# Gate and up blocks of four SwiGLU layers: seven half-size matrix products per pair in place of eight

## The chip, the cores and the metric

The kernel runs on one core of one Trainium2 chip. The metric is device time in microseconds (us), from the first to the last instruction of one execution and what lies around it; lower is better. The engines are called PE (TensorE's matrix products), PEld (its weight loads), DVE (VectorE), ACT (ScalarE), POOL (GpSimd) and SP (which only issues transfers here).

## What is computed

Two blocks of two layers each run one after the other on a sequence of 512 tokens with 1,024 features. Each of the four layers is a mixer (recurrent or attention), in the first block also a cross-attention to a memory, and a SwiGLU layer, each followed by a layer norm. The change touches the four SwiGLU layers alone:

```python
D_MODEL, SEQ, FFN_HIDDEN = 1024, 512, 2816

def swiglu(x, w_gu, w_down):
    gate, up = jnp.split(x @ w_gu, 2, axis=-1)
    return (jax.nn.silu(gate) * up) @ w_down

# in every layer
x = layer_norm(ALPHA * x + swiglu(x, w_gu[layer], w_down[layer]), g, b)
```

All arithmetic is to float32 accuracy.

## The kernel before

**Data.** Activations lie transposed: eight tiles of 128 features by 512 tokens (`XF` in float32, and the same split in two reduced-precision parts `XH` and `XL`, whose sum is `XF`). A gate or up block is 1,024 features by 128 outputs, 512 KB, stored as one 128 x 1024 tile: eight 128 x 128 pieces side by side, one for each tile of x. There are 22 gate and 22 up blocks in a layer (`FT`).

**A product.** `fetch` (L327 to L341) brings a block into `w_raw` (three buffers), ACT rounds it to `w_hi` (L337), and DVE subtracts to get `w_lo` in two halves of 512 columns (L339; four buffers each for `w_hi` and `w_lo`). `mm3` (L271 to L276) then makes three products: high by high, high by low, low by high. So one block is 8 x 3 = 24 matmuls of 128 x 128 by 512 tokens into one PSUM bank.

**A layer.** `ffn` (L549) goes in three parts of 8, 7 and 7 hidden tiles (`FPARTS`). For each hidden tile it computes the gate block into a bank with tag `mm`, the up block into one with tag `sc`, and then `evac`: ACT takes the Silu of gate (L564), DVE multiplies by up (L568), ACT and DVE split the result in `f_h` and `f_l` (L264, L266). Behind each part the down products of that part follow, eight blocks, and are added to `XF` (L404 to L409); those of the last part lie in `close_sublayer`, in two halves of 256 tokens, with the layer norm of the first half under the products of the second. The norm of the second half lies at the start of the next stage: in a SwiGLU layer its first two hidden tiles are computed in two halves of 256 tokens (`halves=True`), while the norm of tokens 256 to 511 is still being finished.

**Order.** The program says what depends on what; when it is built, the framework puts each engine's instructions into one queue, by when it expects them to be ready, and sets the waits between engines. A queue's order is therefore not the program's order, and it is fixed at run time. A buffer's next use waits for the last reader of its former content. `AO` is a scratch area of eight tiles; `close_sublayer` keeps the norm's sums and temporaries there (`room`).

Of the kernel before, what the change touches and what calls it, by code (L numbers as in the profile page):

```python
# [8 lines left out]
F32 = mybir.dt.float32  # L9
F32R = mybir.dt.float32r  # L10
U8 = mybir.dt.uint8
AF = mybir.ActivationFunctionType
ALU = mybir.AluOpType
# [3 lines left out]
P = 128  # L17
S = 512
D = 1024
KT = 8  # L20
# [33 lines left out]
def layout(i):  # L54
# [62 lines left out]
    for l in range(2):  # L117
        ffn(f"f{l}", f["ffn_w_gu"][l], f["ffn_w_down"][l])
        ffn(f"f{l + 2}", f["ffn_w13_2"][l], f["ffn_w2_2"][l])
# [55 lines left out]
def constants():  # L175
    c = {}
    idx = np.arange(P)
    eye = np.eye(P, dtype=np.float32)
    tri_le = (idx[:, None] <= idx[None, :]).astype(np.float32)
    neg_gt = np.where(idx[:, None] > idx[None, :], np.float32(1e30), np.float32(0))  # L180
    neg_lt = np.where(idx[:, None] < idx[None, :], np.float32(1e30), np.float32(0))
    neg_ge = np.where(idx[:, None] >= idx[None, :], np.float32(NEG), np.float32(0))
    tri_lt = (idx[:, None] < idx[None, :]).astype(np.float32)
    tri_ge = -(idx[:, None] >= idx[None, :]).astype(np.float32)
    c["c_sq"] = np.concatenate([eye, neg_gt, neg_lt, neg_ge, tri_lt, tri_ge], axis=1)

    inv = (np.float32(10000.0) ** (-np.arange(0, 64, 2, dtype=np.float32) / np.float32(64))).astype(np.float32)
    ang = np.arange(S, dtype=np.float32)[None, :] * inv[:, None]
    cos, sin = np.cos(ang).astype(np.float32), np.sin(ang).astype(np.float32)
    c["c_rope"] = np.concatenate(  # L190
        [np.concatenate([cos, cos, cos, cos]), np.concatenate([-sin, sin, -sin, sin])], axis=1
    )

    t = np.arange(P)
    lv = np.zeros((P, len(LEVELS), 64), np.float32)
    for n, h in enumerate(LEVELS):
        blk = t // (2 * h)
        right = (t // h) % 2
        lv[:, n, :] = (blk[:, None] == blk[right == 1][None, :]) & (right[:, None] == 0)
    c["c_lv"] = lv.reshape(P, len(LEVELS) * 64)  # L200
    rs = np.ones((P, S), np.float32)
    rs[:, ::64] = 0
    c["c_rs"] = rs
    return c


class Prog:
    def __init__(self, ctx, tc, a):
        self.tc, self.nc, self.a = tc, tc.nc, a
        nc = tc.nc  # L210
        self.cp = ctx.enter_context(tc.tile_pool(name="cst", bufs=1))
        self.st = ctx.enter_context(tc.tile_pool(name="state", bufs=1))
        self.wp = ctx.enter_context(tc.tile_pool(name="wts", bufs=4))
        self.ps = ctx.enter_context(tc.tile_pool(name="ps", bufs=4, space=PSUM))
        st = self.st
        xf = st.tile([P, KT * S], F32, name="xf")
        self.XF = [xf[:, k * S : (k + 1) * S] for k in range(KT)]
        self.all_x = xf.rearrange("p (k s) -> p k s", k=KT)
        self.XH = [st.tile([P, S], F32R, name=f"xh{k}") for k in range(KT)]
        self.XL = [st.tile([P, S], F32R, name=f"xl{k}") for k in range(KT)]  # L220
        self.AO = [st.tile([P, S], F32, name=f"ao{k}") for k in range(KT)]
        cp = self.cp

        ones = cp.tile([P, 2 * P], F32, name="k_ones")
        nc.vector.memset(ones[:, 0:P], 1.0 / D)
        nc.vector.memset(ones[:, P : 2 * P], 1.0 / P)
        self.ones_d, self.ones_p = ones[:, 0:P], ones[:, P : 2 * P]
        nr = cp.tile([P, P], F32R, name="k_nr")
        nc.vector.tensor_scalar(nr, ones[:, P : 2 * P], -float(P), None, ALU.mult)
        self.mones_r = nr  # L230
        pr = cp.tile([P, P], F32R, name="k_pr")
        nc.vector.tensor_copy(pr, ones[:, P : 2 * P])
        self.ones_pr = pr
        cc = cp.tile([P, 4], F32, name="k_cc")
        nc.vector.memset(cc[:, 0:1], LN_EPS)
        nc.vector.memset(cc[:, 1:2], 1.0)
        self.eps, self.one = cc[:, 0:1], cc[:, 1:2]
        self.kv = {}
        self.pending = []
        self.biases = []  # L240
        self.before = []
        self.loaded = False

    def constants(self):
        nc, a = self.nc, self.a
# [22 lines left out]
            y = nc.vector.scalar_tensor_tensor(lo, src, scale, hi.bitcast(F32), ALU.mult, ALU.subtract)  # L268
        return x, y

    def mm3(self, out, w, x, start, stop):  # L271
        nc = self.nc
        (wh, wl), (xh, xl) = w, x
        nc.tensor.matmul(out, wh, xh, start=start, stop=False)  # L274
        nc.tensor.matmul(out, wh, xl, start=False, stop=False)  # L275
        self.last = nc.tensor.matmul(out, wl, xh, start=False, stop=stop)  # L276

    def pair_parts(self, pool, name, width=S):

# [266 lines left out]
        self.close_sublayer(src, self.XH, self.XL, True, ln, keep=keep)  # L546


    def ffn(self, pre, ln, last=False):  # L549
        nc, tc, a = self.nc, self.tc, self.a  # L550
        with tc.tile_pool(name="ffn", bufs=2, reuse_waits="tile") as fp:
            off = 0
            for part, nt in enumerate(FPARTS):
                hs, ls = [], []
                for t in range(nt):
                    hs.append(fp.tile([P, S], F32R, name="f_h", tag="f_h", bufs=11))
                    ls.append(fp.tile([P, S], F32R, name="f_l", tag="f_l", bufs=11))

                def evac(n, ps, c0, c1, keep={}):
                    t = n // 2  # L560
                    c = slice(c0, c1)
                    if n % 2 == 0:
                        s = fp.tile([P, S], F32, name="f_s", tag="f_s", bufs=3)
                        nc.scalar.activation(s[:, c], ps[:, c], AF.Silu)  # L564
                        keep[t, c0] = s
                    else:
                        s = keep.pop((t, c0))
                        nc.vector.tensor_tensor(s[:, c], s[:, c], ps[:, c], ALU.mult)  # L568
                        self.tail = self.split(hs[t][:, c], ls[t][:, c], s[:, c])

                src = []
                for t in range(nt):
                    src += [a[pre + "_gu"][off + t], a[pre + "_gu"][FT + off + t]]
                if part == 0:
                    self.proj_a(src[:4], evac, halves=True)
                    self.proj_a(src[4:], lambda n, ps, c0, c1: evac(n + 4, ps, c0, c1), tags=("mm", "sc"))
                else:
                    self.proj_a(src, evac, tags=("mm", "sc"))
                off += nt
                d = a[f"{pre}_d{part}"]  # L580
                if part < len(FPARTS) - 1:
                    for m in range(8):
                        w = self.fetch(d[m], nt * P)
                        ps = self.mm(("mm", "sc")[m % 2])
                        self.block_a(w, ps, hs, ls)
                        self.add_partial(m, ps, part == 0)
                else:
                    self.close_sublayer([d[m] for m in range(8)], hs, ls, False, ln, last)


# [1011 lines left out]
```

## Time and profile before

| | |
|---|---|
| median of three runs | 2907.42 us (2905.26 to 2908.75) |
| the profiled execution | 2910.26 us, of which 2908.3 us are its span |
| PE busy | 2849.4 us, 98% of the span |
| weight loads (PEld) busy | 2415.0 us, 83% |
| DVE busy | 1694.3 us, 58% |
| ACT busy | 1274.8 us, 44% |
| POOL busy | 424.1 us, 15% |
| mean granted clock of TensorE | 0.996 of full speed |

The busy time of an engine is the time in which at least one of its instructions is running. A matmul's recorded duration is longer than the distance to the next one, since matmuls overlap: the pace is read from the distances between starts. Weight loads run beside the matmuls.

### The profile page before, as it was taken

What the parts mean: (1) busy time and instruction counts of PE and PEld (TensorE: products, weight loads), DVE (VectorE), ACT (ScalarE), POOL (GpSimd) and SP (SyncE); (2) the same over time, 40 slices, a digit from 0 to 9 for tenths busy, and PEclk for the clock granted to TensorE, in tenths of its full rate; (3) what the DMA queues carried; (4) which work ended last, traced back from release to release, by engine and by line L of the source; (5) the groups of instructions that cost most, each with busy time, mean ns of one, the idle gap of its engine ahead of it and who ended that gap; (6) DMA issues with size and microseconds to landing.
All of it is one profiled execution on the core that took longest, in us unless ns stands there. A gap on an engine that the chain in (4) does not pass through costs nothing.

```text
span 2908.3 us, 40029 instructions
## 1 busy us (share of the span) xinstructions
PE 2849.4 (98%) x15354; PEld 2415.0 (83%) x15354; DVE 1694.3 (58%) x3164; ACT 1274.8 (44%) x2328; POOL 424.1 (15%) x500
## 2 busy tenths in 40 slices
PE   9999999999999999999999999999999999999998
PEld 7678989888886678898888988798888976988887
DVE  5877656333469887563333767873333759733335
ACT  4555544222256765442222644652222548532223
POOL 0402012000121121020000432230000302400003
PEclk9999999999999999999999999999999999999999
DMA  5232522333332225223332321223332331133232
GB/s 179 78 117 77 160 66 88 95 98 98 101 97 80 76 70 170 71 80 101 93 99 79 106 73 60 80 88 95 100 96 83 99 93 39 59 103 100 94 94 67
DMA packets 83071, 269.07 MB, mean 93 GB/s; under 512 B 10648, under 2 KB 15144, under 8 KB 82880
## 3 DMA queue, kind: packets, MB, share of 16 engines
q1 hardware_dynamic: 81376, 261.49, 29.3%
q0 software_dynamic: 1504, 5.04, 0.5%
q8 instruction: 120, 1.97, 0.3%
q14 instruction: 71, 0.58, 0.1%
HBM read 260.14 MB, written 2.15 MB: 90 GB/s over the span
## 4 chain that ended last, share of the span: by engine, by line
PE 78%; DVE 13%; ACT 4%; issue 3%; DMA 1%; POOL 0%; SPq 0%; DVEq 0%; ACTq 0%; POOLq 0%
PE p_mm L275 14%; PE p_mm L274 13%; PE p_mm L276 13%; PE p_sc L274 10%; PE p_sc L276 10%; PE p_sc L275 9%; DVE w_lo L339 2%; DVE ao L450 2%; PE p_tp L275 1%; PE p_tp L276 1%; PE p_tp L274 1%; DVE ac L742 1%; DVE xl L460 1%; PE p_sc L1264 1%; DVE ao L449 1%
## 5 line engine op out<-in xcount | busy, mean ns | idle before, releaser
L337 ACT ACTIVATE w_hi<-w_raw 128x1024 fp32r<-128x1024 f32 (+2 forms) x478 | 492.9, 1036 | 1108.6 <-PE p_mm L275 484.1
L339 DVE TENSOR_TENSOR w_lo<-w_raw,w_hi 128x512 fp32r<-128x512 f32 (+2 forms) x956 | 650.1, 710 | 501.9 <-ACT w_hi L337 495.6
L274 PE MATMUL p_mm<-xh,w_hi 128*128 128x512 f32 (+1 forms) x1920 | 688.8, 359 | 7.3 <-ACT w_hi L337 4.9
L275 PE MATMUL p_mm<-xl,w_hi 128*128 128x512 f32 (+1 forms) x1920 | 688.1, 358 | 5.6 <-DVE xl L460 3.6
L276 PE MATMUL p_mm<-xh,w_lo 128*128 128x512 f32 (+1 forms) x1920 | 683.5, 356 | 0.0
L275 PEld LDWEIGHTS p_mm<-xl,w_hi 128*128 128x128 f32 x1920 | 365.2, 190 | 59.0 <-DVE xl L460 6.5
L274 PEld LDWEIGHTS p_mm<-xh,w_hi 128*128 128x128 f32 x1920 | 365.0, 190 | 58.7 <-ACT w_hi L337 4.9
L276 PEld LDWEIGHTS p_mm<-xh,w_lo 128*128 128x128 f32 x1920 | 365.0, 190 | 49.5 <-issue 0.6
L276 PE MATMUL p_sc<-xh,w_lo 128*128 128x512 f32 (+1 forms) x1024 | 358.5, 350 | 0.9 <-DVE w_lo L339 0.9
L274 PE MATMUL p_sc<-xh,w_hi 128*128 128x512 f32 (+1 forms) x1024 | 359.3, 351 | 0.0
L275 PE MATMUL p_sc<-xl,w_hi 128*128 128x512 f32 (+1 forms) x1024 | 358.0, 350 | 0.0
L496 POOL TENSOR_TENSOR ao<-xf 128x256 f32<-128x256 f32 x20 | 19.9, 995 | 1695.6 <-DVE xf L489 1293.8
L568 DVE TENSOR_TENSOR f_s<-f_s,p_sc 128x512 f32<-128x512 f32 x80 | 55.1, 688 | 289.4 <-PE p_sc L276 289.4
L276 PEld LDWEIGHTS p_sc<-xh,w_lo 128*128 128x128 f32 x1024 | 193.7, 189 | 26.4 <-DVE w_lo L339 1.1
L274 PEld LDWEIGHTS p_sc<-xh,w_hi 128*128 128x128 f32 x1024 | 193.6, 189 | 25.8 <-issue 0.4
L275 PEld LDWEIGHTS p_sc<-xl,w_hi 128*128 128x128 f32 x1024 | 193.7, 189 | 25.3 <-issue 0.2
L274 PE MATMUL p_sc<-f_h,w_hi 128*128 128x512 f32 (+1 forms) x464 | 157.5, 339 | 0.0
L276 PE MATMUL p_sc<-f_h,w_lo 128*128 128x512 f32 (+1 forms) x464 | 157.2, 339 | 0.2
L275 PE MATMUL p_mm<-f_l,w_hi 128*128 128x512 f32 (+1 forms) x464 | 157.2, 339 | 0.0
L276 PE MATMUL p_mm<-f_h,w_lo 128*128 128x512 f32 (+1 forms) x464 | 156.7, 338 | 0.0
L274 PE MATMUL p_mm<-f_h,w_hi 128*128 128x512 f32 (+1 forms) x464 | 156.7, 338 | 0.0
L275 PE MATMUL p_sc<-f_l,w_hi 128*128 128x512 f32 (+1 forms) x464 | 156.7, 338 | 0.0
(438 smaller groups left out, 4699.2 us busy)
## 6 DMA issues: line engine op xcount, KB each, us to landing
w_raw<-in_f_gu SPq DMA_DIRECT2D x176, 512.0 KB, 3.5
w_raw<-in_w_e SPq DMA_DIRECT2D x70, 512.0 KB, 3.6
w_raw<-in_w_x SPq DMA_DIRECT2D x64, 512.0 KB, 3.9
w_raw<-in_w_o SPq DMA_DIRECT2D x64, 512.0 KB, 3.7
w_raw<-in_f_d SPq DMA_DIRECT2D x64, 448.0 KB, 3.2
w_raw<-in_f_d SPq DMA_DIRECT2D x32, 512.0 KB, 3.5
r_s<-r_t SPq DMA_DIRECT2D x64, 64.0 KB, 2.0
na_b<-in_na_bias SPq DMA_DIRECT2D x6, 384.0 KB, 3.0
```

The lines of the kernel that those rows point to most:

```text
L274: nc.tensor.matmul(out, wh, xh, start=start, stop=False)
L275: nc.tensor.matmul(out, wh, xl, start=False, stop=False)
L276: self.last = nc.tensor.matmul(out, wl, xh, start=False, stop=stop)
L337: nc.scalar.activation(hi[:, :n], raw[:, :n], AF.Copy)
L339: nc.vector.tensor_tensor(lo[:, c], raw[:, c], hi[:, c].bitcast(F32), ALU.subtract)
L449: eng.tensor_tensor(t, self.XF[m][:, c], mu, ALU.subtract)
L450: nc.vector.scalar_tensor_tensor(t, t, g, r, ALU.mult, ALU.mult)
L460: nc.vector.scalar_tensor_tensor(xl, t, b, xh.bitcast(F32), ALU.add, ALU.subtract)
L496: eng.tensor_tensor(sm, self.XF[order[0]][:, c], self.XF[m][:, c], ALU.add)
L568: nc.vector.tensor_tensor(s[:, c], s[:, c], ps[:, c], ALU.mult)
L742: nc.vector.scalar_tensor_tensor(out, xp[:, j : j + S], w[j], out, ALU.mult, ALU.add)
L1264: nc.tensor.matmul(ps[:, c * 64 : c * 64 + 64].rearrange("p (n h) -> p n h", h=hl), x[:, cs], halves(x[:, cs], hl)[1], start=True, stop=True,)
```

## The change

The first three hidden tiles of each layer stay as they were. The other 19 of 22 (5, 7 and 7 in the three parts) go through the new `seven`. A gate block A1 and its up block A2 are cut into halves of 512 features (A11, A12; A21, A22), x into halves of features and of tokens (B11, B12; B21, B22), and the 2 x 2 product that would need eight half-size products is made of seven:

- sums of weights: S1 = A21 + A22, S2 = S1 - A11, S3 = A11 - A21, S4 = A12 - S2
- sums of x: T1 = B12 - B11, T2 = B22 - T1, T3 = B22 - B12, T4 = B21 - T2
- products: A11 B11, S2 T2, S1 T1, S3 T3, A12 B21, A22 T4, S4 B22

A half-size product is 4 pieces x 3 = 12 matmuls of 128 x 128 by 256 tokens. The sums of x are made once for a layer (`sums_of_x`), in a new allocation of `AO` and in tiles of a pool `fw`; the sums of weights for every pair. Sums and copies are float32, and each is split in a high and a low part as the weights were. One PSUM bank (`pa`) accumulates four products in a row and is copied to SBUF by ACT after the first, the second and the third. `f_s` has two buffers in place of three; `AO` becomes one tile that is allocated anew at two places of each layer. The program begins pair t+1 before it makes the last product of pair t (`yield`).

```diff
+    def new_ao(self, dtype=F32):
+        ao = self.ap.tile([P, KT * S + 16], dtype, name="ao", tag="ao", bufs=1)
+        self.AO = [ao[:, k * S : (k + 1) * S] for k in range(KT)]
+        return ao
...
+    def sums_of_x(self, pool):
+        nc = self.nc
+        pool.tile([P, 48], F32, name="pad_t", bufs=1)
+        b11, b12 = self.all_x[:, 0:4, 0:256], self.all_x[:, 0:4, 256:S]
+        b21, b22 = self.all_x[:, 4:8, 0:256], self.all_x[:, 4:8, 256:S]
+        ts, raws, ao = [], [], self.new_ao(F32R)
+        for n, one in enumerate((b12, b22, b22, b21)):
+            tag = "s12" if n == 1 else "u_raw"
+            raw = pool.tile([P, 1024], F32, name=tag, tag=tag, bufs=2 - n % 2 if n < 2 else 2)
+            raws.append(raw.rearrange("p (k s) -> p k s", k=4))
+            nc.vector.tensor_tensor(raws[n], one, (b11, raws[0], b12, raws[min(n, 1)])[n], ALU.subtract)
+            hi = ao[:, n * 1024 : (n + 1) * 1024]
+            lo = pool.tile([P, 1024], F32R, name=f"t_l{n}", bufs=1)
+            self.split(hi, lo, raw)
+            ts.append([(hi[:, c : c + 256], lo[:, c : c + 256]) for c in range(0, 1024, 256)])
+        return ts
+
+    def seven(self, gate, up, pool, ts, sink):
...
+        def parts(src, n=1024, own=None):
+            if own:
+                hi = pool.tile([P, n], F32R, name=own + "h", tag=own + "h", bufs=1)
+                lo = pool.tile([P, n], F32R, name=own + "l", tag=own + "l", bufs=1)
+            else:
+                hi = self.wp.tile([P, n], F32R, name="w_hi", tag="w_hi", bufs=4)
+                lo = self.wp.tile([P, n], F32R, name="w_lo", tag="w_lo", bufs=4)
+            self.split(hi, lo, src)
+            return hi, lo
+
+        def product(ps, w, c, b, first, last):
+            for k in range(4):
+                ws = slice(c.start + k * P, c.start + (k + 1) * P)
+                self.mm3(ps, (w[0][:, ws], w[1][:, ws]), b[k], first and k == 0, last and k == 3, skip_group_check=not (first and last))
+
+        g = self.wp.tile([P, 1024], F32, name="w_raw", tag="w_raw", bufs=3)
+        u = pool.tile([P, 1024], F32, name="u_raw", tag="u_raw", bufs=2)
+        nc.sync.dma_start(out=g, in_=gate)
+        nc.sync.dma_start(out=u, in_=up)
+        a1 = parts(g)
+        s12 = pool.tile([P, 1024], F32, name="s12", tag="s12", bufs=1)
+        nc.vector.tensor_tensor(s12[:, h1], u[:, h1], u[:, h2], ALU.add)
+        nc.vector.tensor_tensor(s12[:, h2], s12[:, h1], g[:, h1], ALU.subtract)
+        ss = parts(s12, own="s_")
+        nc.vector.tensor_tensor(u[:, h1], g[:, h1], u[:, h1], ALU.subtract)
+        a2 = parts(u)
+        nc.vector.tensor_tensor(g[:, h2], g[:, h2], s12[:, h2], ALU.subtract)
+
+        pa = self.mm("sc")[:, 0:256]
+        pz = self.mm("tp")[:, 0:256]
+        pb = self.mm("mm")[:, 0:256]
...
+        product(pa, a1, h1, b11, True, False)
+        nc.scalar.activation(keep[0], pa, AF.Copy)
+        yield
+        product(pa, ss, h2, t2, False, False)
+        nc.scalar.activation(keep[1], pa, AF.Copy)
+        product(pz, ss, h1, t1, True, False)
+        product(pa, a2, h1, t3, False, False)
+        nc.scalar.activation(keep[2], pa, AF.Copy)
+        nc.vector.tensor_tensor(c22, keep[2], pz, ALU.add)
+        product(pb, a1, h2, b21, True, True)
+        nc.vector.tensor_tensor(s[:, c0], keep[0], pb, ALU.add)
+        nc.scalar.activation(s[:, c0], s[:, c0], AF.Silu)
+        product(pa, a2, h2, t4, False, True)
+        nc.vector.tensor_tensor(s[:, c0], s[:, c0], pa, ALU.mult)
+        a4 = parts(g[:, h2], 512, own="s4")
+        yield
+        product(pz, a4, h1, b22, False, True)
+        nc.vector.tensor_tensor(s[:, c1], keep[1], pz, ALU.add)
+        nc.scalar.activation(s[:, c1], s[:, c1], AF.Silu)
+        nc.vector.tensor_tensor(s[:, c1], s[:, c1], c22, ALU.mult)
+        sink(s)
...
-                    self.proj_a(src[4:], lambda n, ps, c0, c1: evac(n + 4, ps, c0, c1), tags=("mm", "sc"))
-                else:
-                    self.proj_a(src, evac, tags=("mm", "sc"))
+                    fw = extra.enter_context(tc.tile_pool(name="fw", bufs=1, reuse_waits="tile"))
+                    ts = self.sums_of_x(fw)
+                    self.proj_a(src[4:6], lambda n, ps, c0, c1: evac(n + 4, ps, c0, c1), tags=("mm", "sc"))
+                    done = 3
+                before = None
+                for t in range(done, nt):
+                    def sink(s, t=t):
+                        self.tail = self.split(hs[t], ls[t], s)
+                    now = self.seven(src[2 * t], src[2 * t + 1], fw, ts, sink)
+                    next(now)
+                    if before:
+                        next(before, None)
+                    next(now)
+                    before = now
+                next(before, None)
```

## Rows read from the trace of the kernel before

**Rows 1.** The page: span; busy us (share of the span) xinstructions of each engine.
```profile
span 2908.3 us, 40029 instructions
PE 2849.4 (98%) x15354; PEld 2415.0 (83%) x15354; DVE 1694.3 (58%) x3164; ACT 1274.8 (44%) x2328; POOL 424.1 (15%) x500
```

**Rows 2.** Windows: us, busy of PE, PEld, DVE, ACT, POOL, clock, DMA share, GB/s.
```profile
469.00:480.50 11.50, 11.10 (x91) 10.69 (x90) 7.45 (x13) 7.06 (x12) 0.32 (x1) 1.00 0.29 86
491.40:545.00 53.60, 53.60 (x238) 44.41 (x237) 19.38 (x30) 15.75 (x20) 0.00 (x0) 1.00 0.32 93
```

**Rows 3.** Timeline (start, us, instruction): first, last matmul of a 512-token block, next one.
```profile
703.56 0.39 PE L274 MATMUL p_mm<-xh,w_hi 128*128 128x512 f32 x1
...
708.77 0.39 PE L276 MATMUL p_mm<-xh,w_lo 128*128 128x512 f32 x1
709.00 0.39 PE L274 MATMUL p_sc<-xh,w_hi 128*128 128x512 f32 x1
```

**Rows 4.** The same for a 256-token block, and one of its weight loads.
```profile
474.73 0.28 PE L274 MATMUL p_tp<-xh,w_hi 128*128 128x256 f32 x1
...
477.49 0.28 PE L276 MATMUL p_tp<-xh,w_lo 128*128 128x256 f32 x1
477.61 0.28 PE L274 MATMUL p_tp<-xh,w_hi 128*128 128x256 f32 x1
474.74 0.19 PEld L275 LDWEIGHTS p_tp<-xl,w_hi 128*128 128x128 f32 x1
```

**Rows 5.** Timeline of DVE: end of a pair; two 256-column instructions back to back.
```profile
714.71 0.69 DVE L568 TENSOR_TENSOR f_s<-f_s,p_sc 128x512 f32<-128x512 f32 x1 [3.30 <-PE p_sc L276]
715.56 0.69 DVE L339 TENSOR_TENSOR w_lo<-w_raw,w_hi 128x512 fp32r<-128x512 f32 x1 [0.16 <-ACT w_hi L337]
716.17 0.69 DVE L266 TENSOR_TENSOR f_l<-f_s,f_h 128x512 fp32r<-128x512 f32 x1
716.77 0.69 DVE L339 TENSOR_TENSOR w_lo<-w_raw,w_hi 128x512 fp32r<-128x512 f32 x1
...
442.71 0.41 DVE L485 SCALAR_TENSOR_TENSOR xf<-xf,p_mm 128x256 f32<-128x256 f32 x1
443.04 0.47 DVE L460 SCALAR_TENSOR_TENSOR xl<-ao,k_lnp,xh 128x256 fp32r<-128x256 f32 x1
```

**Rows 6.** Timeline of ACT in the same stretch.
```profile
709.02 1.06 ACT L337 ACTIVATE w_hi<-w_raw 128x1024 fp32r<-128x1024 f32 x1 [4.38 <-PE p_mm L275]
709.99 0.58 ACT L564 ACTIVATE f_s<-p_mm 128x512 f32<-128x512 f32 x1
```

**Rows 7.** Groups by line and shape: ... xcount | busy us, mean ns | idle before.
```profile
L438 ACT ACTIVATE ao<-p_sc 128x256 f32<-128x256 f32 x20 | 7.5, 377 | 6.3 <-PE p_sc L435 6.3
L264 ACT ACTIVATE f_h<-f_s 128x512 fp32r<-128x512 f32 x88 | 55.6, 631 | 43.0 <-DVE f_s L568 42.9
L568 DVE TENSOR_TENSOR f_s<-f_s,p_sc 128x512 f32<-128x512 f32 x80 | 55.1, 688 | 289.4 <-PE p_sc L276 289.4
```

**Rows 8.** Timeline where the last part's down products begin, first layer.
```profile
779.49 0.39 PE L276 MATMUL p_sc<-xh,w_lo 128*128 128x512 f32 x1
779.72 0.28 PE L274 MATMUL p_mm<-f_h,w_hi 128*128 128x256 f32 x1
779.99 0.69 DVE L568 TENSOR_TENSOR f_s<-f_s,p_sc 128x512 f32<-128x512 f32 x1 [8.80 <-PE p_sc L276]
780.71 0.63 ACT L264 ACTIVATE f_h<-f_s 128x512 fp32r<-128x512 f32 x1 [5.57 <-DVE f_s L568]
781.38 0.69 DVE L266 TENSOR_TENSOR f_l<-f_s,f_h 128x512 fp32r<-128x512 f32 x1 [0.70 <-ACT f_h L264]
781.87 0.28 PE L274 MATMUL p_mm<-f_h,w_hi 128*128 128x256 f32 x1
782.12 0.39 PE L275 MATMUL p_mm<-f_l,w_hi 128*128 128x256 f32 x1
```

**Rows 9.** Timeline of ACT: the norm's last write of x in a SwiGLU layer.
```profile
470.86 0.90 ACT L454 ACTIVATE xf<-ao,k_lnp 128x256 f32<-128x256 f32 x2
```

More of the change, by code (lines that the diff above doesn't have):

```diff
@@ L212, in __init__ @@
         self.st = ctx.enter_context(tc.tile_pool(name="state", bufs=1))
+        self.ap = ctx.enter_context(tc.tile_pool(name="aos", bufs=1))
         self.wp = ctx.enter_context(tc.tile_pool(name="wts", bufs=4))
@@ L220, in __init__ @@
         self.XL = [st.tile([P, S], F32R, name=f"xl{k}") for k in range(KT)]
-        self.AO = [st.tile([P, S], F32, name=f"ao{k}") for k in range(KT)]
+        st.tile([P, 48], F32, name="pad_a")
+        self.new_ao()
         cp = self.cp
@@ L269, in split, with mm3 @@
         return x, y
-    def mm3(self, out, w, x, start, stop):
+    def mm3(self, out, w, x, start, stop, **kw):
         nc = self.nc
         (wh, wl), (xh, xl) = w, x
-        nc.tensor.matmul(out, wh, xh, start=start, stop=False)
-        nc.tensor.matmul(out, wh, xl, start=False, stop=False)
-        self.last = nc.tensor.matmul(out, wl, xh, start=False, stop=stop)
+        nc.tensor.matmul(out, wh, xh, start=start, stop=False, **kw)
+        nc.tensor.matmul(out, wh, xl, start=False, stop=False, **kw)
+        self.last = nc.tensor.matmul(out, wl, xh, start=False, stop=stop, **kw)
     def pair_parts(self, pool, name, width=S):
@@ new lines, in seven @@
+    def seven(self, gate, up, pool, ts, sink):
+        nc = self.nc
+        t1, t2, t3, t4 = ts
+        x = [[(self.XH[k][:, c], self.XL[k][:, c]) for k in range(4 * i, 4 * i + 4)] for i in range(2) for c in (slice(0, 256), slice(256, S))]
+        b11, b12, b21, b22 = x
+        h1, h2 = slice(0, 512), slice(512, 1024)
+        def parts(src, n=1024, own=None):
[26 more added lines that the diff above has]
+        pb = self.mm("mm")[:, 0:256]
+        keep = []
+        for name, bufs in (("k1", 1), ("k2", 2), ("k3", 1)):
+            keep.append(pool.tile([P, 256], F32, name=name, tag=name, bufs=bufs))
+        s = self.fp.tile([P, S], F32, name="f_s", tag="f_s", bufs=2)
+        c22 = pool.tile([P, 256], F32, name="c22", tag="c22", bufs=1)
+        c0, c1 = slice(0, 256), slice(256, S)
+        product(pa, a1, h1, b11, True, False)
[19 more added lines that the diff above has]
+        sink(s)
@@ L549, in ffn @@
     def ffn(self, pre, ln, last=False):
         nc, tc, a = self.nc, self.tc, self.a
-        with tc.tile_pool(name="ffn", bufs=2, reuse_waits="tile") as fp:
+        with tc.tile_pool(name="ffn", bufs=2, reuse_waits="tile") as fp, ExitStack() as extra:
+            self.fp = fp
             off = 0
@@ L562, in evac @@
                     if n % 2 == 0:
-                        s = fp.tile([P, S], F32, name="f_s", tag="f_s", bufs=3)
+                        s = fp.tile([P, S], F32, name="f_s", tag="f_s", bufs=2)
                         nc.scalar.activation(s[:, c], ps[:, c], AF.Silu)
@@ L573, in ffn @@
                     src += [a[pre + "_gu"][off + t], a[pre + "_gu"][FT + off + t]]
+                done = 0
                 if part == 0:
                     self.proj_a(src[:4], evac, halves=True)
-                    self.proj_a(src[4:], lambda n, ps, c0, c1: evac(n + 4, ps, c0, c1), tags=("mm", "sc"))
-                else:
-                    self.proj_a(src, evac, tags=("mm", "sc"))
+                    fw = extra.enter_context(tc.tile_pool(name="fw", bufs=1, reuse_waits="tile"))
[13 more added lines that the diff above has]
+                next(before, None)
                 off += nt
@@ L587, in ffn @@
                 else:
+                    extra.close()
+                    self.new_ao()
                     self.close_sublayer([d[m] for m in range(8)], hs, ls, False, ln, last)
```

## The prediction, made before the changed kernel was run

> **What bounds the kernel now.** I read the page first. TensorE (PE) is busy for 98% of the span, DVE for 58%, ACT for 44% [rows 1]: what counts is how long PE's queue is, and a saving on PE is worth its full size as long as no other engine takes over. [...]
>
> [...] A block of 24 matmuls over 512 tokens goes from 703.56 to 709.00: 5.44 us, 0.2267 each [rows 3]. The kernel already has stages with 256 tokens per matmul, and there the same 24 go from 474.73 to 477.61: 2.88 us, 0.120 each [rows 4]. Half the columns therefore cost 53% of the time, not 50%.
>
> **PE's part.** A pair has 2 x 24 = 48 matmuls of 512 tokens: 48 x 0.2267 = 10.88 us. After: 7 products x 12 = 84 matmuls of 256 tokens: 84 x 0.120 = 10.08 us. The eighth that is left out would be 1.36 us; the dearer half-size matmul takes 0.56 of it back, 0.80 us a pair remain. There are 19 such pairs in a layer and four layers: 76 x 0.80 = **60.8 us** saved. In [rows 4] each matmul also has its own weight load, 0.19 us long and yet hidden at a distance of 0.120, so more loads per column are already in the 0.120.
>
> [...]
>
> **DVE's part.** Now DVE has six instructions of 512 columns a pair (four `w_lo` halves, the product with up, `f_l`). After it has, for a pair: three low parts of 1024 columns (a1, ss, a2); four sums of weights, one low part of the last sum and one low part of the hidden tile, six of 512; and five of 256 (c22, two adds, two products). A 512-column instruction lasts 0.69 us, but the next starts 0.61 us behind it (715.56, 716.17, 716.77); a 256-column one lasts 0.41 and is followed after 0.33 [rows 5]. From these two, 256 more columns cost 0.27 to 0.28, so 1024 columns take an estimated 1.15 to the next start and 1.23 in duration. Back to back: 3 x 1.15 + 6 x 0.61 + 5 x 0.33 = 8.8 us; with no overlap at all: 3 x 1.23 + 6 x 0.69 + 5 x 0.42 = 9.9 us. I take 9.0, since only a few of the sums read what the instruction before them wrote. Either way it is less than PE's 10.08, but 87 to 98% of it in place of 36%: DVE has nearly no room left.
>
> [...]
>
> What would a late DVE hold up? Its results with one buffer are the nearest to PE. The parts of ss can be overwritten once S1 T1 is done, 5.8 us into the pair, and are wanted by S2 T2 of the next, 7.2 us later; they take 1.06 on ACT [rows 6] and 1.2 on DVE. The parts of S4 have 8.6 us from the last reader to the next, those of a1 and a2 a whole pair. So single delays of 4 to 5 us are covered, and if DVE falls behind it catches up, as its work is shorter than the period. Steady state: PE-bound, no term.
>
> **ACT's part.** Three roundings of 1024 at 1.06, two of 512 at 0.63, three copies of 256 from PSUM at 0.38, two Silus of 256 at about 0.4 [rows 6, 7]: 6.4 us of 10.08. It is not a bound, but its copies stand between two products on one bank: `pa` may not be added to before it is copied. Between them lies a product on another bank, 1.44 us of cover. A handoff costs what a matmul's end is late (0.28 - 0.12), about 0.1 to start, 0.38 to copy and 0.1 back: 0.7 us, covered. But ACT is in order, and `f_s` in [rows 6] started at 709.99 although its bank was complete at 709.2, because a 1.06 us rounding had begun just before. Such a delay makes the handoff 1.7, 0.3 more than the cover. Bounds: 0, and 76 x 3 x 0.3 = 68 us if it met every copy. Roundings are a third of ACT's time and only their first part is long enough: I take **3 us**.
>
> **First pair of each part.** There no older pair's product lies between A11 B11 and S2 T2. Uncovered, that is about 0.7 us, 12 times: 8 us; nothing if S1 T1 is queued first. DVE's queue mixes lines by readiness (`f_l` lies between the halves of a `w_lo` in [rows 5]), PE's may too. I take the middle, **4 us**.
>
> **Sums of x.** Four subtractions and four low parts of 1024: 8 x 1.15 = 9.2 us on DVE, once a layer. They can start when the norm has written x, at 471.8 [rows 9], and are wanted by S2 T2 of the first new pair: halves end at 480.5, the third tile at 491.4, one product more, 492.9. In these 21.1 us DVE also has two blocks' `w_lo` (2.4), two tiles' products and low parts (2.4) and a1, S1, S2, ss of the first pair (3.6): 17.6. It fits by 3.5 us. Bounds 0 and 4 x 9.2 = 37; I take 0.5 a layer, **2 us**.
>
> **End of the last part.** Today the last up block is followed by product, rounding, low part; PE's seventh down piece is ready 0.13 us late (782.12 for 781.99) [rows 8]. The chain gets longer: from the last matmul's end 0.11, add 0.42, Silu 0.4, product 0.42, rounding 0.63, low part 0.69, and some 0.06 for each handoff make 3.1 us against 2.3 of cover by six down pieces of 0.36. So 0.7 more, four times: **3 us**. In the other parts the pieces take 0.68 each, six of them 4.1 us: covered. The new `AO` and pool `fw` are freed by products that lie before the down products: nothing.
>
> **Transfers** keep their number and size (2 x 512 KB a pair); DMA's share is 0.32 in the stage [rows 2]. SP's queue is not moved past anything that PE needs sooner. `f_s` with two buffers is freed a period before it is wanted.
>
> **Sum.** -60.8 + 3 + 4 + 2 + 3 = -48.8 us. The profiled execution's span of 2908.3 becomes 2859.5; its own time is 2910.26, 2.84 above the median of the runs, so the median becomes 2907.42 - 48.8, about **2858 us**. Its own range, all four terms from nothing to a multiple: 2846 to 2885.
>
> **Rivals.**
> *VectorE becomes the bound* (the other side). Five DVE instructions of a pair wait for a product and five for a rounding, and DVE's queue is in order. Where it waits for ACT today it stands 0.16 us [rows 5], after that the next cannot overlap: with 9.9 us of durations and 10 such waits of 0.2, a pair takes 11.9 us, 1.05 more than the 10.88 of before: 76 x 1.05 = +80, 2987 us. It decides from 10.7 us a pair (10.88 less the 12 us of other terms over 76 pairs). For it: 87 to 98% load. Against: buffers leave DVE 4 us ahead, and ready instructions overlap. 12%.
> *The copies of `pa` are not covered.* At half of all copies, 34 us: 2858 - 3 + 34 = 2889. For it: f_s's wait in [rows 6]; against: the long roundings are released by other products than those that the copies follow. 10%.
> *The sums of x hold up PE*: DVE's queue takes the weights or the hidden tiles first, all 9.2 us come late: 2858 - 2 + 37 = 2893. 6%.
> [...] 2%.
>
> **Chances.** My forecast 70%. Faster by over 0.2% (6 us; the three runs lie within 0.12%) are the forecast and most of the second to fourth rival: 81%. Within 0.2%, between those and the first: 6%. Slower: the first rival, and both handoff and sums together: 13%. The range must hold 80%: the forecast's own and the two rivals at 2889 and 2893: 2844 to 2895.
>
> **What would show it.** PE's groups p_sc, p_tp and p_mm with 128x256 at 0.120 between starts, and about 10.1 us a pair (first product to first product); DVE 85 to 95% busy in that stage; PE's idle time before S2 T2 (released by ACT's copies) under 0.1 us a pair. I am wrong if PE shows gaps in every pair that DVE releases (`s_l`, `s4l`, `w_lo`), if the pair takes over 10.7 us, or if PE stands at the first new pair for the low parts of T.

## The result: faster by 2.2%, 13 us more than forecast

The changed kernel takes 2844.85 us (2842.0 to 2846.26, four runs) beside 2906.56 us of the kernel before; the ratio is 0.9783, with a 95% interval of 0.9771 to 0.9795. The forecast was 2858 us: the direction held, PE stayed the bound, and the gain was larger, 62 us by these medians in place of 49. That is 1 us below the forecast's own range (2846 to 2885) and just inside the wider one (2844 to 2895).

The page of the changed kernel, for [rows 1]:

```profile
span 2844.2 us, 46816 instructions
PE 2775.4 (98%) x18090; PEld 2480.9 (87%) x18090; DVE 2120.7 (75%) x3804; ACT 1517.0 (53%) x2800; POOL 423.6 (15%) x500
```

PE is still the bound, at the same 98% of a shorter span; DVE went from 58% to 75%. Windows of the stage that changed, for [rows 2] (us; busy PE, PEld, DVE, ACT, POOL; clock, DMA share, GB/s): three pairs of the first part, the block in which the norm ends, and the last part's first down block:

```profile
500.62:530.26 29.64, 29.64 (x254) 29.64 (x253) 26.56 (x43) 18.35 (x31) 0.00 (x0) 1.00 0.31 108
...
466.68:474.28 7.60, 6.09 (x51) 5.89 (x49) 7.54 (x10) 4.75 (x8) 1.32 (x2) 1.00 0.01 2
762.00:765.32 3.32, 2.98 (x23) 2.64 (x22) 1.79 (x4) 2.17 (x4) 0.00 (x0) 1.00 0.00 0
```

In the pairs PE never stands idle, DVE is busy for 90% and ACT for 62%, at a clock of 1.00. Three pairs take 29.64 us, 9.88 each, where 10.08 was forecast. PE's timeline shows where the 0.20 lies; these are the first matmuls of the products of one pair and of the next, twelve matmuls apart:

```profile
492.73 0.28 PE L283 MATMUL p_tp<-ao,s_h 128*128 128x256 f32 x1
493.92 0.38 PE L283 MATMUL p_sc<-ao,s_h 128*128 128x256 f32 x1 [0.91 <-ACT k L627]
...
510.50 0.28 PE L283 MATMUL p_sc<-xh,w_hi 128*128 128x256 f32 x1
511.93 0.28 PE L283 MATMUL p_tp<-xh,s4h 128*128 128x256 f32 x1
513.28 0.28 PE L283 MATMUL p_sc<-ao,s_h 128*128 128x256 f32 x1
514.72 0.28 PE L283 MATMUL p_tp<-ao,s_h 128*128 128x256 f32 x1
516.16 0.28 PE L283 MATMUL p_sc<-ao,w_hi 128*128 128x256 f32 x1
517.57 0.28 PE L283 MATMUL p_mm<-xh,w_hi 128*128 128x256 f32 x1
519.00 0.29 PE L283 MATMUL p_sc<-ao,w_hi 128*128 128x256 f32 x1
520.38 0.28 PE L283 MATMUL p_sc<-xh,w_hi 128*128 128x256 f32 x1
```

Twelve matmuls with the parts of S1 or S2 (`s_h` against `ao`, which now holds the sums of x) take 1.44 us, 0.120 each, as in [rows 4]. Those with S4 (`s4h`) take 1.35, 0.113; the other four products 1.38 to 1.43. So the half-size matmul has no one price here: it depends on which tiles it reads. The first two rows are the first pair of a layer, where S2 T2 waits 0.91 us for a copy of `pa`. DVE and ACT there, and DVE at the start of the layer and in a steady pair:

```profile
468.60 1.21 DVE L571 TENSOR_TENSOR u_raw<-xf 128x1024 f32<-128x1024 f32 x1
469.74 1.26 DVE L469 SCALAR_TENSOR_TENSOR xl<-ao,k_lnp,xh 128x256 fp32r<-128x256 f32 x3
...
492.96 0.63 ACT L273 ACTIVATE f_h<-f_s 128x512 fp32r<-128x512 f32 x1 [2.59 <-DVE f_s L668]
493.50 0.37 ACT L627 ACTIVATE k<-p_sc 128x256 f32<-128x256 f32 x1
...
507.52 1.23 DVE L275 TENSOR_TENSOR s_l<-s,s_h 128x1024 fp32r<-128x1024 f32 x1 [0.63 <-ACT s_h L273]
508.66 0.41 DVE L634 TENSOR_TENSOR c<-k,p_tp 128x256 f32<-128x256 f32 x1
508.99 0.68 DVE L609 TENSOR_TENSOR s<-u_raw 128x512 f32<-128x512 f32 x1
509.59 0.41 DVE L636 TENSOR_TENSOR f_s<-k,p_mm 128x256 f32<-128x256 f32 x1
```

Two things are to be seen. At 468.60 the first subtraction for the sums of x stands in DVE's queue ahead of the norm's last three low parts of x, which PE is waiting for. And the starts on DVE lie closer than the durations, as in [rows 5]: 1.14 us behind 1024 columns, 0.60 behind 512, 0.33 behind 256. By these a pair's fourteen instructions are 3 x 1.14 + 6 x 0.60 + 5 x 0.33 = 8.67 us; the forecast had taken 9.0.

### The profile page after: what moved, and what is told of

Read it like the earlier page. It is cut to its first block, busy times and chain, and to the rows that moved or that the text cites. A ratio compares the mean times of both kernels' runs of the same rounds, so it can differ in the third digit from the quotient of the medians.

```text
span 2844.2 us, 46816 instructions
## 1 busy us (share of the span) xinstructions
PE 2775.4 (98%) x18090; PEld 2480.9 (87%) x18090; DVE 2120.7 (75%) x3804; ACT 1517.0 (53%) x2800; POOL 423.6 (15%) x500
## 4 chain that ended last, share of the span: by engine, by line
PE 74%; DVE 17%; ACT 4%; issue 3%; DMA 1%; POOL 0%; SPq 0%; DVEq 0%; ACTq 0%; POOLq 0%
PE p_sc L283 10%; PE p_sc L285 10%; PE p_mm L284 10%; PE p_mm L283 10%; PE p_sc L284 10%; PE p_mm L285 10%; PE p_tp L284 4%; PE p_tp L285 4%; PE p_tp L283 4%; DVE w_lo L348 3%; DVE ao L459 2%; DVE ac L859 1%; DVE xl L469 1%; PE p_sc L1381 1%; PE p_sc L333 1%
## 5 line engine op out<-in xcount | busy, mean ns | idle before, releaser
L348 DVE TENSOR_TENSOR w_lo<-w_raw,w_hi 128x512 fp32r<-128x512 f32 (+2 forms) x652 | 450.1, 722 | 205.3 <-ACT w_hi L346 199.2
L284 PE MATMUL p_mm<-xl,w_hi 128*128 128x256 f32 (+1 forms) x1616 | 535.6, 332 | 10.6 <-DVE xl L469 8.8
L283 PE MATMUL p_mm<-xh,w_hi 128*128 128x256 f32 (+1 forms) x1616 | 536.5, 332 | 8.1 <-ACT w_hi L346 5.6
L285 PE MATMUL p_mm<-xh,w_lo 128*128 128x256 f32 (+1 forms) x1616 | 531.4, 329 | 0.0
L284 PEld LDWEIGHTS p_mm<-xl,w_hi 128*128 128x128 f32 x1616 | 307.2, 190 | 39.8 <-DVE xl L469 10.7
L283 PE MATMUL p_sc<-xh,w_hi 128*128 128x256 f32 (+1 forms) x720 | 208.8, 290 | 0.0
L285 PE MATMUL p_sc<-xh,w_lo 128*128 128x256 f32 (+1 forms) x720 | 207.7, 288 | 0.0
L284 PE MATMUL p_sc<-xl,w_hi 128*128 128x256 f32 (+1 forms) x720 | 207.0, 288 | 0.0
L283 PE MATMUL p_sc<-ao,w_hi 128*128 128x256 f32 x608 | 170.2, 280 | 0.0
L284 PE MATMUL p_sc<-t_l,w_hi 128*128 128x256 f32 x608 | 169.8, 279 | 0.0
L285 PE MATMUL p_sc<-ao,w_lo 128*128 128x256 f32 x608 | 169.6, 279 | 0.0
L275 DVE TENSOR_TENSOR s_l<-s,s_h 128x1024 fp32r<-128x1024 f32 x76 | 93.1, 1225 | 64.1 <-ACT s_h L273 64.1
```

What stands on the lines that cost most here:

```text
L275: y = nc.vector.tensor_tensor(lo, src, hi.bitcast(F32), ALU.subtract)
L283: nc.tensor.matmul(out, wh, xh, start=start, stop=False, **kw)
L284: nc.tensor.matmul(out, wh, xl, start=False, stop=False, **kw)
L348: nc.vector.tensor_tensor(lo[:, c], raw[:, c], hi[:, c].bitcast(F32), ALU.subtract)
```

## The experiments

| kernel | median us | ratio to before, 95% |
|---|---|---|
| no_pads | 2860.21 | 0.9818 to 0.9848 |
| opposite | 2848.48 | 0.9775 to 0.9804 |
| eight | 2956.09 | 1.0148 to 1.0179 |
| dve_two | 2849.54 | 0.9780 to 0.9812 |
| dve_four | 2999.11 | 1.0295 to 1.0326 |
| start | 2847.84 | 0.9775 to 0.9805 |
| x_moved | 2844.55 | 0.9730 to 0.9800 |
| x_moved_start | 2843.82 | 0.9758 to 0.9791 |
| after_again | 2843.14 | 0.9766 to 0.9793 |
| ss_moved | 2840.41 | 0.9753 to 0.9779 |
| ss_moved_first | 2836.84 | 0.9741 to 0.9768 |

**Theory and rivals.** The diff holds three pads that the prediction never priced: 48 floats before `ao`, 16 floats at its end, and 48 floats before the low parts of the sums. In the program's addresses, x, `w_hi` and `w_lo` start 32 bytes into a 256-byte line, in both kernels; the pads put the sums of x (high and low parts) and the parts of S1, S2 and S4 at 224. These offsets are worked out from the program's allocations, and no trace shows an address; what the diff shows is the shift, 48 floats of 4 bytes, 192 bytes. Theory: this offset sets the pace of a half-size matmul. Rivals: the mix of seven products is quicker of itself; or PE's pace is as forecast and the other terms were too large.

**The pads left out** (`no_pads`).

```diff
-        st.tile([P, 48], F32, name="pad_a")
...
-        ao = self.ap.tile([P, KT * S + 16], dtype, name="ao", tag="ao", bufs=1)
+        ao = self.ap.tile([P, KT * S], dtype, name="ao", tag="ao", bufs=1)
...
-        pool.tile([P, 48], F32, name="pad_t", bufs=1)
```

> The three small pads are left out, so every tile that a matmul reads starts at byte 32 of a 256-byte line (with the pads AO, the low parts of T, and the parts of ss and S4 start at byte 224, the weights a1 and a2 and x at 32). Placement theory: a half-size matmul takes 0.120 us when its weights and its moving operand start at the same place of a line and 0.113 to 0.117 when they don't; then all seven products go at 0.120, a pair takes 10.08 us in place of 9.88, and the kernel 15 us more than the changed one: about 2860 (0.984 of before). Rival, that short products on alternating banks are quicker wherever the tiles lie: the pair stays at 9.88 and the time at 2845 (0.979).

It took 2860.21 us. PE's timeline, from the product with S4 to that of the next pair:

```profile
510.58 0.28 PE L282 MATMUL p_tp<-xh,s4h 128*128 128x256 f32 x1
512.02 0.28 PE L282 MATMUL p_sc<-ao,s_h 128*128 128x256 f32 x1
...
520.66 0.28 PE L282 MATMUL p_tp<-xh,s4h 128*128 128x256 f32 x1
```

Now S4's product takes 1.44 as well, and the pair 10.08 us: exactly the forecast's 84 x 0.120, and the time is 2 us from the forecast's 2858. The work is the same and so are the waits (the block in which the norm ends takes 7.57 us, the last part's first down block 3.32); the other addresses alone are worth 15 us. The rival of the quicker mix is refuted by this run, and that of a pace as forecast by the 9.88 us of the changed kernel.

**Eight half-size products** (`eight`): the kernel before, with the same 19 pairs a layer in two halves of 256 tokens; no sums, no seventh product saved.

```diff
-                self.block_a(w, ps, self.XH, self.XL)
+                for c in ((0, 256), (256, S)) if cut and n >= cut else ((0, S),):
+                    self.block_a(w, ps, self.XH, self.XL, *c)
...
```

> The kernel before, with the same 19 of 22 pairs of each layer in eight half-size products: each block is computed in two halves of 256 tokens, no sums, no copies. It prices the smaller matmul alone. By the 0.120 us of half-size matmuls on these operands a pair takes 96 x 0.120 = 11.52 us, 0.64 more than in 512-token matmuls: 76 x 0.64 = 49 us more, about 2955 (1.017 of before). Rival, that the gain comes from going in halves (0.1176 each as in the mix of the changed kernel): 11.29 us a pair, 2938 (1.011), or if from a quicker pipeline, no more than 2907 (1.000).

It took 2956.09 us, as expected: 48 more than before (2908.38 in these runs). One block of 24, PE's timeline:

```profile
520.55 0.28 PE L274 MATMUL p_sc<-xh,w_hi 128*128 128x256 f32 x1
...
523.43 0.28 PE L274 MATMUL p_mm<-xh,w_hi 128*128 128x256 f32 x1
```

2.88 us for 24, 0.120 each; a pair is 4 x 2.88 = 11.52, 0.64 more than the 10.88 of before, and 76 x 0.64 = 49. So cutting the products in half costs, by itself, what the forecast charged for it, and the gain is that of the eighth product left out.

**Weights at the other offset** (`opposite`): the pads so placed that all split weights start at 224 and x, its sums and the hidden tiles at 32.

```diff
+        self.wp.tile([P, 48], F32, name="pad_w", bufs=1)
...
-        st.tile([P, 48], F32, name="pad_a")
...
```

> Other pads: all split weights (from fetch, ss, S4) start at byte 224 of a 256-byte line, and x, the sums of x, the hidden tiles and the memory's tiles at byte 32, in every stage that computes in halves of 256 tokens. Placement theory: ss with T and a1 with x (0.119 to 0.120 in the changed kernel) come to 0.113 to 0.117, a pair to 9.5 to 9.8 us (84 matmuls at 0.113 to 0.117), so 6 to 27 us less; and the other half-size matmuls of the kernel, some 4,850, gain up to 0.007 us each, 32 us. About 2790 to 2815 (0.960 to 0.969). Rival (banks, not places): 2845 (0.979).

It took 2848.48 us. By its time this is the rival (2845, a ratio of 0.979), but the rival says that the place does not matter, and PE's timeline shows that it does. One pair, and the first matmuls of two 512-token blocks:

```profile
510.51 0.28 PE L283 MATMUL p_sc<-xh,w_hi 128*128 128x256 f32 x1
511.92 0.28 PE L283 MATMUL p_tp<-xh,s4h 128*128 128x256 f32 x1
...
520.40 0.28 PE L283 MATMUL p_sc<-xh,w_hi 128*128 128x256 f32 x1
...
547.10 0.39 PE L283 MATMUL p_sc<-f_h,w_hi 128*128 128x512 f32 x1
...
552.60 0.39 PE L283 MATMUL p_mm<-f_h,w_hi 128*128 128x512 f32 x1
```

All seven products run at 0.118 (1.41 for twelve), the pair takes 9.89 us, by coincidence what the changed kernel's mix takes, and the 512-token matmuls have become dearer: 5.50 for a block of 24, 0.229 each, for 5.44 in [rows 3]. The theory in its simple form (another offset: 0.113) fell; what stood was that weights at another offset than x make half-size matmuls cheaper and full-size ones dearer.

**x at the other offset** (`x_moved`): x and its sums and the hidden tiles at 224, all weights at 32.

```diff
+        st.tile([P, 48], F32, name="pad_x")
         self.XH = [st.tile([P, S], F32R, name=f"xh{k}") for k in range(KT)]
...
+            fp.tile([P, 48], F32, name="pad_f", bufs=1)
```

> The changed kernel with its padding put elsewhere: x (both parts), its sums and the hidden tiles start 224 bytes into a 256-byte line, all weights 32 bytes into one. This is the placement of the memory tiles in the trace of before, whose 256-token matmuls come every 0.1135 us. If the offset of what moves against the weights sets the pace, all half-size matmuls come at 0.1135: a pair takes 9.53 us for 9.88 (76 x 0.35 = 27), the other 256-token blocks (about 4,800 matmuls) save 31 us: about 2790. Rival, from the kernel with the weights moved: the mix settles at 0.1175 whatever the offset, 2840 to 2850.

The median, 2844.55, is the rival's, but the profiled execution took 2824.46 and the other three 2842.05 to 2848.3. PE's timeline of the profiled one: a product and a 512-token block in the first layer, and the same product in the second:

```profile
518.51 0.28 PE L283 MATMUL p_tp<-xh,s4h 128*128 128x256 f32 x1
519.87 0.28 PE L283 MATMUL p_sc<-ao,s_h 128*128 128x256 f32 x1
...
537.55 0.39 PE L283 MATMUL p_mm<-f_h,w_hi 128*128 128x512 f32 x1
543.15 0.39 PE L283 MATMUL p_sc<-f_h,w_hi 128*128 128x512 f32 x1
...
1382.58 0.28 PE L283 MATMUL p_tp<-xh,s4h 128*128 128x256 f32 x1
1383.99 0.28 PE L283 MATMUL p_sc<-ao,s_h 128*128 128x256 f32 x1
```

In the first layer the half-size products take 1.36, 0.1133 each, as expected, and a pair 9.52 us; the full-size blocks take 5.60, 0.2333, which takes back a part of it. But at 1382.58, with the same offsets and the same granted clock of 1.00 (0.996 over the whole execution), the product takes 1.41, 0.118 each, as in `opposite`. Each pace holds for whole parts of a layer: 59 of the 76 pairs lie in parts at 9.52 us a pair, and 17 (two parts of the second layer, one of the fourth) in parts at 9.89.

A third kernel has the same placement and the edits of order of `start` (below):

> The two edits of order and the moved x together. If both hold and don't meet: 10 us less than with the moved x alone, about 2780. If the moved x gives nothing, as the time with the edits of order alone, about 2835.

It took 2843.82, and neither number came. Its trace has both paces too: the first part of each layer goes at 9.52 us a pair, the second and third at 9.89. From one S4 product to the next in the second part:

```profile
614.50 0.28 PE L283 MATMUL p_tp<-xh,s4h 128*128 128x256 f32 x1
...
624.39 0.28 PE L283 MATMUL p_tp<-xh,s4h 128*128 128x256 f32 x1
```

Where the offsets differ, they do not fix the pace: 0.1133 and 0.118 stand side by side in one execution. An estimate from the pairs alone: with its 59 quick pairs at 9.89, the profiled execution of `x_moved` would have taken 22 us more, about 2846, in the midst of the other three. That these ran mostly at the slower pace is argued from this, not shown, since they have no trace.

**S1 and S2 moved alone** (`ss_moved`): in the changed kernel the two products at 0.120 are those whose weights and sums of x both start at 224. Two pads put S1 and S2 at 32 and leave all else.

```diff
+        pool.tile([P, 16], F32, name="pad_s", bufs=1)
         return ts
...
+                if own == "s4":
+                    pool.tile([P, 48], F32, name="pad_4", tag="pad_4", bufs=1)
```

> The changed kernel with two more pads: the parts of S1 and S2 start 32 bytes into a 256-byte line in place of 224, where the sums of x they are multiplied with stay; S4 stays at 224, x and all other weights at 32. If a half-size product runs at 0.120 only where weights and x have the same offset, the two products with S1 and S2 fall from 0.120 to the 0.113 to 0.117 of the others: 24 x 0.003 to 0.007 a pair, 76 pairs, 5 to 12 us: 2833 to 2840. The 512-token matmuls, all at 32 and 32, stay at 0.2277. Rival: the offset of the product before or the parity of the loads decides, and the time stays at 2843 to 2847.

2840.41 us, at the upper end of what was expected and below the rival's 2843; the changed kernel itself, run beside it (`after_again`), took 2843.14. The single runs overlap (2837.16 to 2843.81 and 2842.21 to 2848.37), but the traces differ in every pair: 9.83 us in place of 9.88. Of `after_again` had been expected:

> The changed kernel as it is, beside the two above on the same chip: 2842 to 2847 again, for the comparison with them.

With one edit more (`ss_moved_first`), S1 T1 queued ahead of S2 T2 in the first pair of a layer:

```diff
+        if alone:
+            product(pz, ss, h1, t1, True, False)
+            with self.tc.issue_after(self.last.ins):
+                product(pa, ss, h2, t2, False, False)
...
```

> The same, and in the very first pair of a layer alone S1 T1 is queued ahead of S2 T2, the sums of x where they were. In the run with both edits of order that took 1.1 us of idle time from that place and gave 0.3 to 0.4 back behind it; the wait at the third tile, which came from the later sums, should not come back: 4 x 0.7 = 3 us less than without it.

2836.84 us, the lowest median of all, 3.6 less than `ss_moved`. Its PE timeline, the two products with S2 and S1 of a pair and, ahead of them, the first pair:

```profile
492.24 0.29 PE L283 MATMUL p_tp<-ao,s_h 128*128 128x256 f32 x1
...
493.78 0.39 PE L283 MATMUL p_sc<-ao,s_h 128*128 128x256 f32 x1
...
512.67 0.28 PE L283 MATMUL p_sc<-ao,s_h 128*128 128x256 f32 x1
514.09 0.28 PE L283 MATMUL p_tp<-ao,s_h 128*128 128x256 f32 x1
515.50 0.28 PE L283 MATMUL p_sc<-ao,w_hi 128*128 128x256 f32 x1
```

1.41 to 1.42 for twelve where it was 1.44: 0.05 us a pair, 4 us in 76, while x against weights at 32, untouched, stays at 0.120 in the halves and 0.2267 in the down blocks. In the first pair S1 T1 now fills the wait for the copy. From that pair's first matmul to the next pair's it is 9.27 to 9.29 us, for 9.51 to 9.66 in `ss_moved`: 0.2 to 0.4 a layer, some 1.2 us in four. Where the rest of the 3.6 comes from is not shown.

**More work on DVE** (`dve_two`, `dve_four`): the low parts of a1 and a2 written twice, and three times.

```diff
             self.split(hi, lo, src)
+            for _ in range(times - 1):
+                nc.vector.tensor_tensor(lo, src, hi.bitcast(F32), ALU.subtract)
...
```

> The changed kernel, in which VectorE makes the low parts of a1 and of a2 twice (the second time over the same result): 2 x 1.15 = 2.3 us more on VectorE for each of the 76 pairs, nothing else. Theory of the prediction (VectorE is second, with about 1 us of room in a pair, and catches up from its queue): 8.8 to 9.0 + 2.3 = 11.1 to 11.3 us a pair, VectorE becomes the bound, 1.2 to 1.4 us above 9.88: 91 to 107 us more, 2936 to 2952 (1.010 to 1.016). Rival, waits in VectorE's queue were already dominant and the added work falls into them: under 20 us more, below 2865 (0.986). Other rival, every wait of its queue adds: 12 us a pair or more, above 3000.

> The changed kernel, with the low parts of a1 and of a2 each written three times over: 4.56 us more on VectorE in a pair, 13.2 in place of 8.67. By the prediction's rival VectorE sets the pair from there on: 76 x (13.2 - 9.9) = +250, about 3095 us. By what the two extra low parts showed (10.95 us a pair of 9.88, and next to no loss), VectorE works ahead while the down products run and the runs of 5 or 7 pairs end before its lead is used up: with some 8 us of lead a part, 4 x (9 + 15 + 15) = +160 us, 2960 to 3040. If VectorE had still more room than that, under 2900.

With 8.67 + 2 x 1.14 = 10.95 us of DVE a pair, more than the pair takes, the kernel took 2849.54: some 5 us lost, not 90 and more. A window of `dve_two` over most of the seven pairs of the second part:

```profile
593.00:657.00 64.00, 64.00 (x539) 63.66 (x539) 63.46 (x99) 37.46 (x63) 0.00 (x0) 1.00 0.30 103
```

DVE is busy for 63.46 of 64 us, and PE still for all of them. With 13.2 us a pair it took 2999.11. PE's timeline of `dve_four` in the same part, starts of S4's product, pair by pair:

```profile
619.41 0.28 PE L283 MATMUL p_tp<-xh,s4h 128*128 128x256 f32 x1
...
629.29 0.28 PE L283 MATMUL p_tp<-xh,s4h 128*128 128x256 f32 x1
...
652.12 0.28 PE L283 MATMUL p_tp<-xh,s4h 128*128 128x256 f32 x1
...
665.94 0.28 PE L283 MATMUL p_tp<-xh,s4h 128*128 128x256 f32 x1
```

This part's first pairs still come every 9.88 us, the later ones every 13.82: DVE had prepared the first pairs' weights while the down products ran (its `s_l` at 574.75 and `w_lo` at 584.13, ahead of the part's first product at 599.33), and the later pairs wait for it. With 10.95 us a pair the second and third parts end before such a lead is used up (all distances in them are 9.88), and the first parts lose 0.5 us; with 13.2 every part comes to slow pairs. So what decides is not DVE's work against PE's in one pair, but how far it falls behind over five or seven pairs. The step of the rival, that it decides from 10.7 us a pair, is refuted.

**Order at the start** (`start`): in the changed kernel the subtractions are queued behind the norm's last low part, and S1 T1 ahead of S2 T2 in the first pair of all three parts.

```diff
+            with self.tc.issue_after(self.normed.ins):
+                nc.vector.tensor_tensor(raws[n], one, ..., ALU.subtract)
...
```

> The changed kernel with two edits of order and none of work: VectorE's subtractions for the sums of x are queued behind the norm's last low part of x, and in the first pair of each part S1 T1 is queued ahead of S2 T2. If the 0.9 us that PE loses in the block at 466.68 comes from the sum queued ahead of the norm, and the 1.1 to 1.2 us before the first S2 T2 (and 0.3 in the other two parts) from the uncovered copy, each layer saves 0.9 + 1.1 + 0.6 = 2.6 us: 2845 - 10 = 2835. Rival: the waits move on to the next late thing (the low parts of T, or the copy of the other bank), and the time stays at 2843 to 2846.

2847.84: no gain, as the rival had it. Windows of the block in which the norm ends, and of the third hidden tile's start, and the timeline of DVE and PE there:

```profile
468.11:474.83 6.72, 6.32 (x50) 5.92 (x49) 6.53 (x9) 3.68 (x7) 1.30 (x2) 1.00 0.01 2
480.59:482.77 2.18, 1.14 (x5) 0.39 (x3) 2.18 (x4) 1.85 (x2) 0.00 (x0) 1.00 0.27 36
```

```profile
471.48 2.35 DVE L572 TENSOR_TENSOR u_raw<-xf 128x1024 f32<-128x1024 f32 x2
...
479.76 2.35 DVE L275 TENSOR_TENSOR t_l<-u_raw,ao 128x1024 fp32r<-128x1024 f32 x2
482.04 0.68 DVE L348 TENSOR_TENSOR w_lo<-w_raw,w_hi 128x512 fp32r<-128x512 f32 x1
...
481.55 0.50 PE L283 MATMUL p_sc<-xh,w_hi 128*128 128x512 f32 x1 [0.33 <-ACT w_hi L346]
482.77 0.50 PE L285 MATMUL p_mm<-xh,w_lo 128*128 128x512 f32 x1 [0.72 <-DVE w_lo L348]
```

The block fell from 7.60 to 6.72 us, so the cause named for the 0.9 us was right. But from 471.48 DVE has no break, and the third tile's `w_lo` starts at 482.04, when PE has long been there: PE loses 1.6 us in the third tile (12.53 us from 480.59 to the first pair, for 10.90 in the changed kernel). The other edit gained little: from a part's first matmul to the next pair's it is 8.93 us in a layer's first part, for 9.68, but 9.0 in the two others, for 8.78. The waits were moved, not removed: the 9.2 us of sums have to stand in front of something.

## Why the prediction came out 13 us too high

**The step that failed is the pair: "84 x 0.120 = 10.08 us".** Its terms by the trace: 76 x (10.88 - 9.88) = 76 us saved, not 60.8. The price of [rows 4] is that of a block whose x and weights start at the same offset, and the pads of the diff put the new operands elsewhere. `no_pads` gives 10.08 us a pair and 2860 us: with the price for the placement that was assumed, the sum holds within 2 us. The forecast's own range left this price no room: its lower end, 2846, is the sum with the four other terms at nothing. The fourth rival, a half-size matmul cheaper in this mix than in [rows 4], had the right kind of effect, and was given 2 in 100. No row that was printed has a lower price, but the trace of before has one, in a block where memory tiles (at 224 by the program's addresses) meet weights at 32 (PE's timeline, 21 matmuls apart):

```profile
295.15 0.28 PE L274 MATMUL p_sc<-mm_h,w_hi 128*128 128x256 f32 x1
...
297.53 0.28 PE L274 MATMUL p_mm<-mm_h,w_hi 128*128 128x256 f32 x1
```

2.38 us for 21 is 0.1133, and of the 256-token blocks with weights only those with memory tiles have that pace there. In the changed pair S4's product is at 0.113, the two of a2 with sums of x at 0.115 and 0.118, the two of x with unpadded weights at 0.118 to 0.119, and those of S1 and S2 at 0.120: 9.88 in all, and none lower than 0.113.

**The other terms** came to about the 12 us of the forecast, but by other shares, so that their sum agrees is luck:
- *ACT's copies* (3 us): nothing in steady pairs, where PE never stands idle; 52 distances from one pair's S4 product to the next's are 9.87 to 9.89 us, and 12 are 8.46, ahead of each part's last, before which no further pair's first product lies.
- *First pair of each part* (4 us): about 6.6. In the first part the copy at 493.50 stood behind the rounding of `f_h` at 492.96, and PE lost 1.15 us with what follows (9.68 us to the next pair's first matmul, where a steady pair without S4's product takes 8.53); in the two others 0.25 each (8.78). The mechanism, ACT's order, is the one named; only a third of S1 T1 got ahead.
- *Sums of x* (2 us): about 3.6, by another mechanism. The low parts of T were ready in time; it was the first subtraction, queued ahead of the norm, that cost 0.9 a layer (the block takes 7.60 us, and 6.71 in the trace of before). Room was as small as reckoned: in `start` the sums, queued later, held up the third tile instead.
- *End of the last part* (3 us): 3.32 us for the first down block, against 2.74 from 779.72 to 782.46 in the trace of before: 0.58 a layer, 2.3 in all. The chain was as described: it ends with `f_l`, which starts at 764.23.

Sum: 76 - 0 - 6.6 - 3.6 - 2.3 = 63.5 us; the spans differ by 64.1.

**DVE** was busy for 90% of the stage (85 to 95 forecast), and was not the bound. "Nearly no room left" was right for one pair and wrong for the stage, as `dve_two` shows. The fourteen instructions of a pair take 8.67 us by the measured starts, close to the 9.0 that was taken: behind an instruction of 0.68 us the next that stood ready started after 0.60, so the forecast's 9.9 with no overlap was not reached.

**The alignment.** The pace of a half-size matmul was 2 to 6% quicker (0.118 to 0.1133 us, for 0.120) where weights and moving operand differ in offset.

**Still open:** why the offset matters, and what makes the pace change between 0.1133 and 0.118 when offsets differ. In the second layer of `x_moved` it changes across the third tile's full-size blocks (0.1133 up to 1265.60, 0.118 from 1276.78) with no idle time of PE between. Offsets other than 32 and 224 were not tried, so that 256 bytes are the line that counts is not shown either.

## What to carry to other kernels

Before pricing an instruction by a row, make sure that the row reads operands laid out like the new ones: pads in a diff are part of the change (here worth 15 us, `no_pads`), and a second row with another price is worth looking for. An engine at 90% of a stage is not near to setting the time if the stage is short and the engine can work ahead through the next (in `dve_two` DVE was busy for 63.46 of 64 us, and some 5 us were lost); count how far it falls behind over the whole run of iterations. When a wait is moved by order alone, look first for what then stands behind it.

## What the runs showed of the hardware

- The pace of a 128 x 128 matmul with 256 columns of these operands was 0.120 us when weights and moving operand started at the same offset in a 256-byte line (32 and 32, or 224 and 224; 0.118 to 0.119 in the two products of a changed pair that read x and a1), and 0.113 to 0.118 when one was at 32 and the other at 224. With 512 columns it was the other way round: 0.2267 at the same offset, 0.229 (`opposite`: weights at 224) and 0.2333 (`x_moved`: moving operand at 224) at different ones. The granted clock was 1.00 in the pairs of the changed kernel, of `no_pads` and of `opposite`.
- At the same offset the pace of 0.120 came back in the 256-token blocks of the traces of before, the changed kernel, `eight` and `ss_moved_first`; at different offsets one execution held both 0.1133 and 0.118, each for whole parts of a layer (`x_moved`, 59 pairs and 17; `x_moved_start`, 20 and 56).
- Float32 instructions with two inputs that stood ready in DVE's queue started 1.14 us behind one of 1024 columns that lasts 1.23, 0.60 behind 512 (0.68), 0.33 behind 256 (0.41), in the changed kernel.
